# Steps of the RWKV preparation further apart in TensorE's order, key factors ahead of the norm, token mix on ScalarE and VectorE

## The chip, the core and the metric

One core of a Trainium2 chip runs one program. The metric is the device time of one execution in microseconds. Times of parts come from one profiled execution, whose trace names each instruction by its engine and its source line. TensorE (PE) multiplies, VectorE (DVE) and ScalarE (ACT) work on tiles in SBUF and PSUM, GpSimd (POOL) on tiles in SBUF; SyncE (SP) issues the transfers.

## The reference, cut to what matters

One decoder layer over 1024 tokens of width 1024. A normalised input is projected with one wide matrix; its columns feed a windowed attention, an RWKV-7 time mixing and two gates. The part that the change touches is the time mixing:

```python
pr = pr + (pr_prev - pr) * mix            # token mix of r, k, v (pr_prev: the token before)
a = sigmoid(a0 + a_low @ a_up)
kk = k * k_k;  kk = kk / max(norm(kk), 1e-12)      # per head of 64
k = k * (1 + (a - 1) * k_a)
# per token t, per head: S = S diag(decay) + (S @ -kk) (kk*a)^T + v k^T;  y = S @ r
```

The other branch, the merge and the output norm follow, and nothing in them changes.

## The kernel before, in words

The kernel runs in stages: norm and transposition of the input, the RWKV stage (about 97 to 590 us of the trace), attention by head pairs, and the output projections. All large products are made of three fp32r matmuls (high and low halves), hence the lines `acc<-hh,whi`, `acc<-hl,whi`, `acc<-hh,wlo`; their line in the profile is that of the helper `mm`, L140 (transposes: `tr`, L146).

**The RWKV stage** runs the recurrence in 8 segments of 128 tokens, each of two chunks of 64. For each segment there is a preparation (`rwkv_prep`), a rows part (`rwkv_rows`), the chain over the two chunks (`rwkv_chain`, six steps, which depend on one another) and a post part (`rwkv_post`). All are generators: one `next` emits one step. TensorE has a third kind of work in this stage, the projections of spans, gates and of attention-independent columns, cut into units (`run(n)` emits n of them): a unit is one matmul of 512 columns, or two of 256 while the spans last. They fill the time between the dependent steps.

**The order.** While `self.pinned` is set, `mm` and `tr` keep TensorE's instructions in program order, so the order in which `rwkv` calls `next` and `run` is TensorE's order, written out by hand in `PROLOGUE`, `SLOTS` and `FILLS`. The instructions of the other engines and the transfers are not pinned: a planner that simulates the timeline when the kernel is built places them on their queues, and each engine then works in that order. The chain's steps have high priority in it.

In segment i the letters of `SLOTS` mean: `t`, `e`, `a`, `b` the next step of the preparation of segment i, i+1, i+2 and i+3; `f` the rows of segment i+1; `h` the post part of segment i-1. Each slot is one step of the chain, then its letters, then its units (18 in the first six segments, then 14, then 10).

**The steps of a preparation**, between its `yield`s (L498 to L599 and L626 to L668):

1. Load `r` and `k` with the token before (`raw`, L506), mix: POOL subtracts (L508, into tag `cm`), VectorE multiplies and adds (L510), once per head pair.
2. Matmuls of the low-rank codes into two PSUM buffers (`pg`), ScalarE's `tanh` of them (L525: `sig`, `aa`); VectorE's scan of the decay (L530), `kk` and its square `q` on ScalarE (L536, L537).
3. Eight matmuls `pg<-hs,q` for the norms; the power -0.5 on POOL (L545).
4. Transposition of the norms.
5. `pg<-rt,selp`, which spreads the norms; `kk` scaled (L554), exponentials (L558 to L560), `ar` and `bk` on POOL and VectorE (L564 to L571), `k` with its factor (L569, L570), `bw` (L578).
6. and 7. Gram matmuls `pg<-ar,bk` for head pairs 0, 1 and 2, 3: 64 small matmuls into both `pg` buffers, which VectorE masks into `gt` (L592). Step 7 also mixes `v` and sends the blocks of `gt` through DRAM for the inversion of 16x16 blocks on VectorE (`rwkv_blocks`, L601).
8. to 11. The rest of the inverse (`rwkv_inverse`), on `pi` tiles: `pi<-xt,gt`, `pi<-xd,xq`, and the two of 32x32.

The pool `ps_g` of the `pg` tiles has two buffers, and `raw` has two; `k`, `aa`, `cm`, `c` and `bk` have one.

In segment i, `b` makes step 1 of the preparation of segment i+3, `a` steps 2 to 7 of that of i+2, `e` steps 8 to 10 and `t` step 11. In `SLOTS` steps 2 and 3 (`taafh`) follow each other directly, and so do 6 and 7 (`eaa`).

Of the kernel before, what the change touches and what calls it, by code (L numbers as in the profile page):

```python
# [10 lines left out]
F32 = mybir.dt.float32  # L11
# [6 lines left out]
P = 128  # L18
# [5 lines left out]
NPAIR = 4  # L24
# [19 lines left out]

PROLOGUE = (("0", 24), ("0", 10), ("0", 10), ("0", 8), ("0", 44), ("0", 4), ("0", 4), ("1", 12), ("1", 16), ("1", 12),
            ("f", 4), ("f", 4), ("1", 8), ("1", 24), ("0", 8), ("0", 8), ("0", 8), ("1", 0), ("1", 6), ("0", 6), ("2", 0),
            ("f", 8))
SLOTS = ("taafh", "af", "ah", "ef", "eaa", "eb")
FILLS = 6 * [6 * [18]] + [6 * [14], 6 * [10]]
# [61 lines left out]
class Kernel:  # L111
# [233 lines left out]
    def rwkv(self):  # L345
# [5 lines left out]
        with ExitStack() as ctx:  # L351
# [13 lines left out]
            nc.vector.tensor_scalar(self.k_a1, self.k_a, -1.0, 1.0, ALU.mult, ALU.add)  # L365
            self.blk = rc.tile([P, P], F32, name="blk")
# [13 lines left out]
            self.mhalf = rc.tile([P, 1], F32, name="mhalf")  # L380
            nc.vector.memset(self.mhalf, -0.5)
# [40 lines left out]
            def run(n):  # L422
                for _ in range(n):
                    next(fill, None)
# [8 lines left out]
            for i in range(NSEG):  # L433
                chain = self.rwkv_chain(self.segs[i])
                rows = self.rwkv_rows(i + 1) if i + 1 < NSEG else none
                post = self.rwkv_post(self.segs[i - 1]) if i else none
                work = dict(t=prep[i], e=prep[i + 1], a=prep[i + 2], b=prep[i + 3], f=rows, h=post)
                for slot, n in zip(SLOTS, FILLS[i]):
                    with tc.high_priority():
                        next(chain)  # L440
                    for g in slot:
                        next(work[g], None)
                    run(n)
                for n in range(3 * i, 3 * i + 3):
                    self.bias_rows(n)
# [52 lines left out]
    def rwkv_prep(self, s):  # L498
# [5 lines left out]
        def shifted(i, dst):  # L504
            raw = self.rw.tile([P, NPAIR, 1 + SEG], F32, name="raw", tag="raw", bufs=2)
            nc.sync.dma_start(raw, self.raw_d[i].rearrange("p q t -> q p t")[:, :, s * SEG:s * SEG + SEG + 1])  # L506
            d = self.t_("cm")
            nc.gpsimd.tensor_tensor(d, raw[:, :, 0:SEG], raw[:, :, 1:], ALU.subtract)  # L508
            for p in pairs:
                nc.vector.scalar_tensor_tensor(dst[:, p], d[:, p], self.mix[:, 4 * i + p:4 * i + p + 1], raw[:, p, 1:],  # L510
                                               ALU.mult, ALU.add)

        shifted(0, r)
        shifted(1, k)
# [31 lines left out]
        yield  # L546
        self.tr(ps[0:n, 1], rn, self.ident)
        rt = self.rw.tile([n, SEG], F32, name="rt", tag="rt")
        nc.vector.tensor_copy(rt, ps[0:n, 1])
        yield  # L550
        ps = self.ps_g.tile([P, NPAIR, SEG], F32, name="pg", tag="pg")
        for p in pairs:
            self.mm(ps[:, p], self.selp[:, p], rt, start=True, stop=True)
        nc.vector.tensor_tensor(kk, kk, ps, ALU.mult)  # L554

# [5 lines left out]
        nc.vector.tensor_copy(wc, v4(ew)[:, :, :, C - 1:C])  # L561
        ar = self.rw.tile([P, NPAIR, CPS, 2 * C], F32, name="ar", tag="ar", bufs=3)
        bk = self.rw.tile([P, NPAIR, CPS, 2 * C], F32, name="bk", tag="bk")
        nc.gpsimd.tensor_tensor(ar[:, :, :, 0:C], v4(kk), v4(ewm), ALU.mult)  # L564
        nc.gpsimd.tensor_tensor(ar[:, :, :, C:], v4(r), v4(ew), ALU.mult)
        nc.vector.scalar_tensor_tensor(kk, aa, 1.0, kk, ALU.add, ALU.mult)
        nc.vector.scalar_tensor_tensor(bk[:, :, :, 0:C], v4(kk), 0.5, v4(ei), ALU.mult, ALU.mult)
        for p in pairs:
            nc.scalar.activation(aa[:, p], aa[:, p], AF.Identity, bias=col(self.k_a1, p), scale=col(self.k_a, p))  # L569
        nc.gpsimd.tensor_tensor(k, k, aa, ALU.mult)  # L570
        nc.gpsimd.tensor_tensor(bk[:, :, :, C:], v4(k), v4(ei), ALU.mult)  # L571
# [585 lines left out]
```

## Time and profile before

| | us |
|---|---|
| median of three runs | 1474.66 (1471.13 to 1475.28) |
| the profiled execution's own time | 1473.51 |
| its span, first to last instruction | 1471.7 |
| TensorE busy in the span | 1346.3 (91%) |
| VectorE, ScalarE, POOL busy | 795.6, 550.6, 505.3 |
| mean granted TensorE clock | 0.959 |

The time lies 1.8 us above the span, for what is before the first and after the last instruction. An engine's busy time is the union of its instructions' times; issuing and waiting do not count. A granted clock of 1.00 is 2.4 GHz; 0.5 is 1.2 GHz, and a value between is the mean over a stretch at both. Where a row ends in `[1.78 <-ACT sig L525]`, the engine sat idle 1.78 us before it until ScalarE's instruction of line 525 that writes `sig` released it. The segments' chains start at 195.85, 258.07, 316.06, 371.97, 426.05, 483.25, 534.44 and 569.77 us.

### The profile page before, as it was taken

How to read it: one execution, taken by the hardware profiler on the slowest of the kernel's cores; microseconds unless marked ns; L12 is line 12 of the kernel's file. 1: busy time of each engine (PE TensorE's matmuls, PEld its weight loads, DVE VectorE, ACT ScalarE, POOL GpSimd, SP SyncE). 2: the span in 40 equal slices, each digit the busy share in tenths (PEclk: the TensorE clock that was granted, in tenths of full speed). 3: DMA queues.
4: the chain of work that ended last, by engine and by line, in shares of the span. 5: the costliest groups of instructions: out<-in, count | busy, mean ns of one | idle time of the engine just before them, and what ended most of it. 6: DMA issues, size and time to landing. Idle time of an engine off the chain costs nothing.

```text
span 1471.7 us, 25716 instructions
## 1 busy us (share of the span) xinstructions
PE 1346.3 (91%) x10078; PEld 1139.1 (77%) x10078; DVE 795.6 (54%) x1674; ACT 550.6 (37%) x1282; POOL 505.3 (34%) x402
## 2 busy tenths in 40 slices
PE   4988788978988999999999999899989997998997
PEld 3888678867767778788877888788778886776886
DVE  5312535555555552455567656765576558437623
ACT  4444443534533533244433443354325430002211
POOL 1346635634534533322213221322133215344300
PEclk9999889989999999999999999999999998999999
DMA  8673433323223222311122112211131135565216
GB/s 166 163 225 95 121 85 96 91 65 82 77 62 85 67 67 66 88 51 43 39 61 80 36 40 54 87 39 41 47 81 37 36 113 177 179 188 155 80 29 172
DMA packets 199230, 131.17 MB, mean 89 GB/s; under 512 B 52788, under 2 KB 179340, under 8 KB 199108
## 3 DMA queue, kind: packets, MB, share of 16 engines
q1 hardware_dynamic: 199108, 129.52, 32.2%
q8 instruction: 79, 1.29, 0.4%
q14 instruction: 43, 0.35, 0.1%
HBM read 100.31 MB, written 33.89 MB: 91 GB/s over the span
## 4 chain that ended last, share of the span: by engine, by line
PE 38%; DVE 7%; DMA 6%; issue 3%; ACT 3%; POOL 1%; SPq 0%; DVEq 0%; POOLq 0%; ACTq 0%
PE acc L140 24%; DMA wb<-wd 3%; PE acc L1098 2%; PE acc L1097 2%; PE acc L1099 2%; DMA wstage<-in_w_out_dram 1%; PE pw L944 1%; ACT L L877 1%; PE pw L870 1%; PE pw L869 1%; DVE q L848 1%; PE pv L956 1%; PE pv L958 1%; DVE whi L133 1%; PE acc L783 1%
## 5 line engine op out<-in xcount | busy, mean ns | idle before, releaser
L140 PE MATMUL acc<-hh,whi 128*128 128x512 f32 (+1 forms) x1360 | 475.4, 373 | 26.1 <-DVE kl L857 10.8
L140 PE MATMUL acc<-hh,wlo 128*128 128x512 f32 (+1 forms) x1360 | 480.5, 377 | 3.6 <-POOL wlo L136 3.5
L140 PE MATMUL acc<-hl,whi 128*128 128x512 f32 (+1 forms) x1360 | 471.6, 370 | 0.0
L136 POOL TENSOR_TENSOR wlo<-wstage,whi 128x512 fp32r<-128x512 f32 x186 | 249.6, 1342 | 542.7 <-DVE whi L133 255.5
L140 PEld LDWEIGHTS acc<-hh,whi 128*128 128x128 f32 x1360 | 250.7, 194 | 71.4 <-issue 18.7
L140 PEld LDWEIGHTS acc<-hh,wlo 128*128 128x128 f32 x1360 | 251.6, 195 | 44.7 <-POOL wlo L136 5.3
L140 PEld LDWEIGHTS acc<-hl,whi 128*128 128x128 f32 x1360 | 250.4, 194 | 38.1 <-issue 1.3
L877 ACT ACTIVATE L<-L,nm 128x128 f32<-128x128 f32 (+1 forms) x192 | 83.9, 438 | 84.6 <-DVE nm L874 84.4
L871 DVE CUSTOM_DVE_ANT_0 L<-pw,bias 128x128 f32<-128x128 f32 (+1 forms) x192 | 62.4, 351 | 51.2 <-PE pw L870 50.6
L135 ACT CAST whi<-wstage 128x512 fp32r<-128x512 f32 x78 | 48.3, 619 | 107.2 <-PE acc L140 54.2
L856 POOL CAST k<-k 64x512 fp32r<-64x512 f32 x48 | 48.0, 999 | 104.0 <-ACT k L855 97.9
L133 DVE CAST whi<-wstage 128x512 fp32r<-128x512 f32 x108 | 52.5, 487 | 51.9 <-PE acc L140 33.7
L855 ACT CAST k<-acc 64x512 fp32r<-64x512 f32 x48 | 42.9, 894 | 72.9 <-DVE kl L857 51.5
L847 ACT ACTIVATE q<-acc 64x512 fp32r<-64x512 f32 x48 | 43.9, 915 | 57.7 <-DVE q L848 29.6
L857 DVE TENSOR_TENSOR kl<-acc,k 64x512 fp32r<-64x512 f32 x48 | 45.4, 945 | 31.5 <-ACT k L855 31.1
L848 DVE SCALAR_TENSOR_TENSOR q<-acc,q 64x512 fp32r<-64x512 f32 x48 | 44.8, 934 | 21.3 <-ACT q L847 20.4
L947 ACT CAST ph<-pw 128x512 fp32r<-128x512 f32 x72 | 40.8, 582 | 35.2 <-PE pv L956 20.8
L948 DVE TENSOR_TENSOR pl<-pw,ph 128x512 fp32r<-128x512 f32 x72 | 47.3, 670 | 11.8 <-ACT ph L947 10.4
L870 PE MATMUL pw<-kl,q 128*128 128x128 f32 (+1 forms) x192 | 50.7, 278 | 1.4 <-DVE kl L857 1.4
L1097 PE MATMUL acc<-wo,mh 128*128 128x512 f32 x128 | 49.8, 389 | 0.0
L1098 PE MATMUL acc<-wo,mh 128*128 128x512 f32 x128 | 49.8, 389 | 0.0
L1099 PE MATMUL acc<-wo,ml 128*128 128x512 f32 x128 | 49.6, 389 | 0.0
(226 smaller groups left out, 2191.9 us busy)
## 6 DMA issues: line engine op xcount, KB each, us to landing
wstage<-in_w_in_dram SPq DMA_DIRECT2D x170, 256.0 KB
x<-in_x_dram SPq DMA_DIRECT2D x32, 256.0 KB
raw<-raw_d SPq DMA_DIRECT2D x24, 258.0 KB
raw_d<-rv SPq DMA_DIRECT2D x24, 256.0 KB
wb<-wd SPq DMA_DIRECT2D x24, 256.0 KB
bias_d<-bias_r SPq DMA_DIRECT2D x24, 192.0 KB
tb_d<-tb SPq DMA_DIRECT2D x16, 256.0 KB
ga_d<-tb SPq DMA_DIRECT2D x16, 256.0 KB
```

What stands on the lines that cost most here:

```text
L133: self.nc.vector.tensor_copy(hi, x)
L135: self.nc.scalar.copy(hi, x)
L136: self.nc.gpsimd.tensor_tensor(lo, x, hi.bitcast(F32), ALU.subtract)
L140: ins = self.nc.tensor.matmul(*args, **kw)
L848: nc.vector.scalar_tensor_tensor(self.gview(qs2[h][b], g, half), pv, 0.125, hi.bitcast(F32), ALU.mult, ALU.subtract)
L856: nc.gpsimd.tensor_copy(self.gview(ks2[h][b], g, half), hi.bitcast(F32))
L870: nc.tensor.matmul(ps[:, :w], qs2[h][:, qc], kl[h][:, kc], start=False, stop=True)
L871: nc.vector.tensor_tensor_reduce(l[:, l0:l0 + w], ps[:, :w], self.bias[h][:, bo:bo + w], 1.0, -3.0e38, ALU.add, ALU.max, st[:, gi, 0, h, n ...
L877: nc.scalar.activation(ls, ls, AF.Exp, bias=nm[:, n:n + 1], scale=1.0, accum_out=st[:, gi, 1, h, n:n + 1])
L1097: nc.tensor.matmul(ps, mh[k][:, ts], wh[:, k], start=k == 0, stop=False)
L1098: nc.tensor.matmul(ps, mh[k][:, ts], wl[:, k], start=False, stop=False)
L1099: nc.tensor.matmul(ps, ml[k][t // 4][:, cs], wh[:, k], start=False, stop=k == KT - 1)
```

## The change

It does four things. `SLOTS` becomes `LOOP`, a list of (what, units), where `C` is a step of the chain; the units are multiplied by `FILLS`, 6 in the first six segments, then 5, then 3. The six steps of the chain keep 18 x 6 units per segment between them, and the steps of the preparations are spread over them. In the prologue four units are added ahead of step 7 of the second preparation. In step 1 `k` comes before `r`, and the mix is `(1 - mix) * raw` on ScalarE and then `mix * raw_before + that` on VectorE; POOL's subtraction goes. The exponentials move to step 3, and `k`'s factor (into tag `c`, no longer over `aa`), `k`, its half of `bk` and `r`'s half of `ar` move to step 4, ahead of the spreading of the norms.

```diff
-            ("f", 4), ("f", 4), ("1", 8), ("1", 24), ("0", 8), ("0", 8), ("0", 8), ("1", 0), ("1", 6), ("0", 6), ("2", 0),
+            ("f", 4), ("f", 4), ("1", 8), ("1", 24), ("0", 8), ("0", 8), ("0", 8), ("1", 4), ("1", 6), ("0", 6), ("2", 0),
...
-SLOTS = ("taafh", "af", "ah", "ef", "eaa", "eb")
-FILLS = 6 * [6 * [18]] + [6 * [14], 6 * [10]]
+LOOP = (("C", 0), ("t", 0), ("f", 1), ("a", 1), ("h", 1), ("C", 0), ("f", 1), ("a", 2), ("C", 0), ("a", 1), ("h", 2),
+        ("C", 0), ("a", 1), ("f", 0), ("e", 2), ("C", 2), ("a", 1), ("e", 0), ("C", 1), ("a", 1), ("e", 1), ("b", 0))
+FILLS = 6 * [6] + [5, 3]
...
+            self.mix1 = rc.tile([P, 12], F32, name="mix1")
+            nc.vector.tensor_scalar(self.mix1, self.mix[:, 0:12], -1.0, 1.0, ALU.mult, ALU.add)
...
-                for slot, n in zip(SLOTS, FILLS[i]):
-                    with tc.high_priority():
-                        next(chain)
-                    for g in slot:
+                for g, n in LOOP:
+                    if g == "C":
+                        with tc.high_priority():
+                            next(chain)
+                    else:
                         next(work[g], None)
-                    run(n)
+                    run(n * FILLS[i])
...
-            d = self.t_("cm")
-            nc.gpsimd.tensor_tensor(d, raw[:, :, 0:SEG], raw[:, :, 1:], ALU.subtract)
             for p in pairs:
-                nc.vector.scalar_tensor_tensor(dst[:, p], d[:, p], self.mix[:, 4 * i + p:4 * i + p + 1], raw[:, p, 1:],
-                                               ALU.mult, ALU.add)
-
+                nc.scalar.activation(dst[:, p], raw[:, p, 1:], AF.Copy, scale=self.mix1[:, 4 * i + p:4 * i + p + 1])
+            for p in pairs:
+                nc.vector.scalar_tensor_tensor(dst[:, p], raw[:, p, 0:SEG], self.mix[:, 4 * i + p:4 * i + p + 1],
+                                               dst[:, p], ALU.mult, ALU.add)
+
+        shifted(1, k)
         shifted(0, r)
-        shifted(1, k)
...
-        yield
-        self.tr(ps[0:n, 1], rn, self.ident)
-        rt = self.rw.tile([n, SEG], F32, name="rt", tag="rt")
-        nc.vector.tensor_copy(rt, ps[0:n, 1])
-        yield
-        ps = self.ps_g.tile([P, NPAIR, SEG], F32, name="pg", tag="pg")
-        for p in pairs:
-            self.mm(ps[:, p], self.selp[:, p], rt, start=True, stop=True)
-        nc.vector.tensor_tensor(kk, kk, ps, ALU.mult)
-
         ew, ewm, ei = self.t_("q"), cm, self.t_("sig")
...
         nc.vector.tensor_copy(wc, v4(ew)[:, :, :, C - 1:C])
+        yield
+        self.tr(ps[0:n, 1], rn, self.ident)
+        rt = self.rw.tile([n, SEG], F32, name="rt", tag="rt")
+        nc.vector.tensor_copy(rt, ps[0:n, 1])
         ar = self.rw.tile([P, NPAIR, CPS, 2 * C], F32, name="ar", tag="ar", bufs=3)
         bk = self.rw.tile([P, NPAIR, CPS, 2 * C], F32, name="bk", tag="bk")
+        t = self.t_("c")
+        for p in pairs:
+            nc.scalar.activation(t[:, p], aa[:, p], AF.Identity, bias=col(self.k_a1, p), scale=col(self.k_a, p))
+        nc.gpsimd.tensor_tensor(k, k, t, ALU.mult)
+        nc.gpsimd.tensor_tensor(bk[:, :, :, C:], v4(k), v4(ei), ALU.mult)
+        nc.gpsimd.tensor_tensor(ar[:, :, :, C:], v4(r), v4(ew), ALU.mult)
+        yield
+        ps = self.ps_g.tile([P, NPAIR, SEG], F32, name="pg", tag="pg")
+        for p in pairs:
+            self.mm(ps[:, p], self.selp[:, p], rt, start=True, stop=True)
+        nc.vector.tensor_tensor(kk, kk, ps, ALU.mult)
         nc.gpsimd.tensor_tensor(ar[:, :, :, 0:C], v4(kk), v4(ewm), ALU.mult)
-        nc.gpsimd.tensor_tensor(ar[:, :, :, C:], v4(r), v4(ew), ALU.mult)
         nc.vector.scalar_tensor_tensor(kk, aa, 1.0, kk, ALU.add, ALU.mult)
         nc.vector.scalar_tensor_tensor(bk[:, :, :, 0:C], v4(kk), 0.5, v4(ei), ALU.mult, ALU.mult)
-        for p in pairs:
-            nc.scalar.activation(aa[:, p], aa[:, p], AF.Identity, bias=col(self.k_a1, p), scale=col(self.k_a, p))
-        nc.gpsimd.tensor_tensor(k, k, aa, ALU.mult)
-        nc.gpsimd.tensor_tensor(bk[:, :, :, C:], v4(k), v4(ei), ALU.mult)
```

`mhalf`, the constant -0.5, is also made a few lines earlier.

## Rows read from the trace of the kernel before

**Rows 1.** Table by stretch: us, busy PE, PEld, DVE, ACT, POOL, clock, DMA, GB/s.

```profile
195.85:534.44 338.59, 298.32 (x3765) 255.08 (x3764) 185.18 (x421) 150.12 (x360) 158.54 (x130) 0.90 0.30 78
...
534.44:569.77 35.33, 33.84 (x423) 27.35 (x422) 15.03 (x45) 13.78 (x33) 10.74 (x10) 1.00 0.23 66
614.60:1471.70 857.10, 814.28 (x4092) 678.30 (x4092) 509.93 (x1026) 288.91 (x706) 234.96 (x176) 0.98 0.28 81
```

**Rows 2.** Waits of TensorE, 195.85 to 534.44: us in total, times, longest.

```profile
PE pg L140 <- DVE gt L592: 22.2, 9, 4.5
PE pg L140 <- ACT sig L525: 15.0, 6, 3.2
```

**Rows 3.** Timeline of TensorE, 374 to 380: start, us, instruction, idle before.

```profile
374.54 1.71 PE L140 MATMUL pg<-wa,waup 64*128 64x128 f32 x16
378.03 1.05 PE L140 MATMUL pg<-hs,q 128*128 128x2 f32 x8 [1.78 <-ACT sig L525]
```

**Rows 4.** Timeline of ScalarE, same stretch.

```profile
376.32 0.63 ACT L752 ACTIVATE yt<-d 128x512 f32<-128x512 f32 x1 [0.93 <-DVE d L751]
376.85 1.12 ACT L525 ACTIVATE sig<-pg,vecs 128x128 f32<-128x128 f32 x4
```

**Rows 5.** Timeline of TensorE, 406 to 415.

```profile
406.25 0.68 PE L140 MATMUL upd<-rhs_s,tt 64*64 64x64 f32 x16
406.76 1.10 PE L140 MATMUL pi<-xd,xq 64*64 64x64 f32 x32
407.69 1.17 PE L140 MATMUL pg<-ar,bk 64*64 64x64 f32 x64
412.29 0.33 PE L140 MATMUL pg<-ar,bk 64*64 64x64 f32 x2 [3.43 <-DVE gt L592]
412.89 1.66 PE L140 MATMUL pg<-ar,bk 64*64 64x64 f32 x62 [0.27 <-DVE gt L592]
```

**Rows 6.** Timeline of VectorE, 407 to 413 and 437 to 439.

```profile
407.85 2.13 DVE L510 SCALAR_TENSOR_TENSOR k<-cm,vecs,raw 128x128 f32<-128x128 f32 x4 [1.15 <-POOL cm L508]
...
411.58 1.25 DVE L592 TENSOR_TENSOR gt<-pg,gmask 128x512 f32<-128x512 f32 x2
...
437.61 0.71 DVE L641 STREAM_TRANSPOSE xt<-xd 128x512 f32<-128x512 f32 x1 [1.21 <-DMA xd<-x_d]
```

**Rows 7.** Same table, projection matmuls and users of `acc` alone.

```profile
332.32:336.61 4.29, 4.29 (x18) 3.28 (x18) 0.69 (x1) 0.09 (x1) 1.00 0.16 61
379.67:385.38 5.71, 5.71 (x18) 4.33 (x18) 0.69 (x1) 0.60 (x1) 0.73 0.30 82
...
215.96:220.45 4.49, 4.49 (x36) 4.35 (x36) 0.00 (x0) 0.00 (x0) 1.00 0.45 129
```

**Rows 8.** Groups of TensorE, 97 to 600: busy us, mean ns, idle before.

```profile
L140 PE MATMUL pg<-rt,selp 8*128 8x128 f32 x64 | 9.2, 283 | 0.0
```

**Rows 9.** Tile raw: ns min/median/max of its users; idle time of their engines before them.

```profile
L510 DVE SCALAR_TENSOR_TENSOR r<-cm,vecs,raw x32: 335/1123/1380, 89.1 to 461.7; 128x128 f32<-128x128 f32 x32
...
L508 POOL TENSOR_TENSOR cm<-raw x24: 1040/1042/1547, 88.0 to 510.1; 128x512 f32<-128x512 f32 x24
...
  POOL cm L508: 55.8, 11
  DMA raw<-raw_d: 11.6, 3
```

**Rows 10.** Line L573, a 128x128 product on ScalarE: ns min/median/max.

```profile
L573 ACT ACTIVATE r<-r,vecs x32: 385/387/404, 119.3 to 497.0; 128x128 f32<-128x128 f32 x32
```

**Rows 11.** Timeline of SP's queue and of POOL, from 139.5.

```profile
139.62 0.92 SPq L506 DMA_DIRECT2D raw<-raw_d  x2
...
143.11 1.04 POOL L508 TENSOR_TENSOR cm<-raw 128x512 f32<-128x512 f32 x1 [5.53 <-DMA raw<-raw_d]
```

**Rows 12.** Waits of TensorE, 97 to 195.85.

```profile
PE pg L140 <- ACT q L537: 14.3, 2, 8.6
```

**Rows 13.** Timeline of ScalarE, from 139.5.

```profile
153.50 1.02 ACT L536 ACTIVATE kk<-k,vecs 128x128 f32<-128x128 f32 x3 [6.95 <-DVE k L510]
```

More of the change, by code (lines that the diff above doesn't have):

```diff
@@ L365, in rwkv @@
             nc.vector.tensor_scalar(self.k_a1, self.k_a, -1.0, 1.0, ALU.mult, ALU.add)
+            self.mhalf = rc.tile([P, 1], F32, name="mhalf")
+            nc.vector.memset(self.mhalf, -0.5)
+            self.mix1 = rc.tile([P, 12], F32, name="mix1")
+            nc.vector.tensor_scalar(self.mix1, self.mix[:, 0:12], -1.0, 1.0, ALU.mult, ALU.add)
             self.blk = rc.tile([P, P], F32, name="blk")
@@ L379, in rwkv @@
             nc.vector.tensor_copy(self.selp, ps[0:2 * NPAIR])
-            self.mhalf = rc.tile([P, 1], F32, name="mhalf")
-            nc.vector.memset(self.mhalf, -0.5)
             self.smask = rc.tile([P, NPAIR * SEG], F32, name="smask")
```

## The prediction

> **What bounds the kernel now.** I read the table by stretch first. TensorE does most of the work, so time can only come from its idle gaps or from a slow clock, and the table says where these are. From 614.6 us to the end it is busy 814 of 857 us at a granted clock of 0.98. In the six segments from 195.85 to 534.44 us it is busy 298 of 338.6 us, at 0.90 [rows 1]. The segment after them, in which no preparation step 2 to 7 runs, has 1.5 us of idle time and a clock of 1.00. The list of TensorE's waits names two causes for the six segments [rows 2]: the Gram matmuls behind L592's masking on VectorE (22.2 us in the six segments, nearly one wait a segment, longest 4.5) and the norm's matmuls behind L525's evacuation on ScalarE (15.0, six times, longest 3.2). That is 37.2 us.
>
> Both are places where the fixed order puts a step straight behind the one that feeds it. In the segment from 371.97, step 2's 16 matmuls end at 376.25 and step 3 starts at 378.03 with nothing between them [rows 3]: ScalarE came to `sig` at 376.85, after an `ACTIVATE` of the post step that had waited for VectorE [rows 4]. Step 6's Gram group ends at 408.86, and step 7's waits 3.43 us and again 0.27 [rows 5]. The masking it waits for starts at 411.58, and VectorE spent the time before on the token mix of a later preparation, `k` from 407.85 after 1.15 us on POOL [rows 6], and on three short steps behind it.
>
> A wait costs twice. The same 18 fill units take 4.29 us at granted 1.00 and 5.71 at 0.73, in the stretch just behind the wait of step 3 [rows 7]: part of it ran at the lower level, 1.2 GHz.
>
> **The target.** The segment from 534.44 shows the undisturbed price: 35.33 less its 1.5 us of idle time [rows 1] is 33.83 with 84 units. A full segment has 24 units more, 24 x 0.238 = 5.72, and the steps 2 to 7: 1.71 and 1.05 [rows 3], the norm's spreading 9.2/8 = 1.15 [rows 8], two Gram groups at 1.17 [rows 5]. That makes 45.8. The first two segments' units cost 4.49 a slot, not 4.29 [rows 7], so 1.2 more each. Six segments: 277 of today's 338.6. **At most 62 us** is to be had in them: 37.2 of waits, 25 mostly of slow clock.
>
> **The change, part by part.**
> *Order.* The units per segment stay 18 x 6; the last two segments trade six units (84 to 90, 60 to 54). Nothing is added to TensorE. Between steps 2 and 3 now lie 12 units (2.86), `upd` (0.68 [rows 5]), four transposes and 6 units (1.43): 5.0 us without the transposes, against a longest wait of 3.2. Between steps 6 and 7 lie 6 units, step 9 (1.10 [rows 5]), the chain's third step (two groups of 16 like `upd`, about 1.3, an estimate) and 6 units: 5.3 us against a longest wait of 4.5. Both waits go, the second with less to spare. The chain's own six steps stay 18 units apart. What comes later relative to its use is the block inverse: in today's trace its result is transposed at 437.61, 23 us after the Gram group's end at 414.55 [rows 5, 6]. In the new order 72 units (17.1 us) and some 12 us of small groups (an estimate from their rows) lie before step 8, which reads it, so it stays hidden with some 6 us to spare. Step 7 takes its transfers along on SP's queue, `v`'s load, two stores and four loads of blocks, then four stores and two loads, nearer to step 1's loads. At 0.46 us an issue [rows 11] that is 6 us in 23; the weights are asked for a whole projection ahead, which hides it from TensorE. Without that lead it would cost up to the 6.
> *Key factors ahead of the norm.* They move three POOL products and four ScalarE steps from after the norm's spreading to before it. Step 6 does not wait in the trace, so this is worth nothing by itself; it keeps step 6 safe now that it comes sooner. If POOL took them ahead of the `pow`, step 4's transpose would wait 3 to 5 us (three 128x512 steps at 1.04 to 1.55 [rows 9]) less 4 of cover; the `pow` needs only the norm's matmuls and is ready before the exponentials' users, so I take nothing.
> *Token mix.* Out go 24 POOL subtractions (1.04 to 1.55 us), in come 96 ScalarE products of 128x128 at 0.387 us [rows 9, 10]: 12 a segment, 4.6 us. ScalarE was busy 150 of 338.6 us [rows 1]; it goes to (150 + 28)/283 = 63%. VectorE keeps its 96 steps, but they no longer stand behind POOL, for which it sat idle 55.8 us in all, and the longer of them (median 1.12 us for `r` against a shortest of 0.335 [rows 9]) may shrink. None of this lies on TensorE's path; it takes the token mix's waiting on POOL out of what delays the masking. The raw loads remain 24 and only their order changes, `k` first; SP passes the same queue. A ScalarE product can now stand waiting for a load: about 3.5 us from issue to the first use [rows 11], with the chain's copies behind it. The bounds are nothing and 3.5 us per shift; the chain's steps lie some 6 us apart, so I take nothing on the path but keep 1 us a segment for all such leftovers, 6 us.
> The 96 products are 37 us of ScalarE; if all of it reached TensorE, the sum below would be 1443, which is a harder form of rival 1 and has its chance there. A rule of the Trainium skill speaks for that side: ScalarE: Activation LUTs, Rules for kernel authors, sends multiplies and adds to VectorE, not to ScalarE. The trace does not bear it out for these shapes, since VectorE's own steps of the token mix are the dear ones (median 1.12 us against 0.387).
> *Prologue* (97 to 195.85 us). TensorE waits 14.3 us in two norm steps [rows 12]. The second, 8.6, is on `kk`, for which ScalarE sat idle 6.95 us [rows 13]: `k`'s load is third, behind `v` and `r`, which share two buffers. With `k` ahead of `r` I take 6 us (between 3 and 8.6). The first, 5.7, waits for a load that cannot come earlier; one POOL step less and a better order on ScalarE give 2 (0 to 4.5). Shorter waits return some 3 us of slow clock (2 to 5). Together 11, between 3 and 18.
> *Sum:* 62 - 6 + 11 = 67. The profiled execution took 1473.5 us (span 1471.7), 1.2 below the median of 1474.66. **1473.5 - 67 = 1406 us.** What follows this stage is bound by TensorE and moves up with it.
>
> **The rivals.**
> 1. *ScalarE takes over as the one that is late.* `sig`, `aa`, `kk`, the square, the post step and the products come to some 8 us of it around steps 2 and 3 (two times 1.12, two times 0.63 [rows 4], twelve times 0.387 [rows 10]), and a load's 3.5 us may come on top. If step 3 still waits 2 us a segment and the clock falls with it (1.4 in the fill and about as much in the small groups), 6 x 4.8 = 29 us stay: 1435. For it: today's wait is one of ScalarE's order. Against: 5 us of cover.
> 2. *The masking stays late: the change does not do what it says.* Only TensorE's order is written out; the planner places VectorE's work, and it did put the token mix before the masking [rows 6]. If the masking comes 2 us beyond the cover, 2 us and about 2 of clock in six segments: 1430. Against: POOL's waits in that queue are gone.
> 3. *Slower than before.* ScalarE's products wait for all three loads in a row with the chain's copies behind: 3 x (3.5 + 4 x 0.387) = 15 us less 6 of cover is 9 us of idle TensorE, with 3 of slow clock 12 a segment. In eight segments 96 us, more than the 67: 1406 + 96 = 1502. It decides from about 12 us of blocked ScalarE a segment, where 6 of idle time and 2 of clock, eight times, eat the 67. For it: VectorE stood 55.8 us behind the same loads' users [rows 9], and ScalarE kept its order when `yt` was not ready and `sig` stood behind it [rows 4]. The Trainium skill has this as a rule, in TensorE: Matmul & The Clock Gate, section Architectural detail: ScalarE's queue is a strict FIFO; the trace agrees. Against: the loads were mostly there when POOL came to them (it waited for one 3 times in 24 [rows 9]).
>
> **How the numbers follow.** Forecast 0.62; rival 1 0.16, rival 2 0.10, rival 3 0.04; the rest, in which smaller leftovers add up differently, 0.08. The forecast's own range is 1393 (no leftovers, the prologue's best) to 1420; 7 us below it are left for the later stages, which run at 0.98 [rows 1]. Rivals 1 and 2 reach to 1440, so the range is **1386 to 1440**. Faster by over 0.3% (4.4 us, about what a measurement of this kernel can tell from no change): 0.91; within it 0.04; slower 0.05.
>
> **What would show it.** Right: in the changed profile the two rows of TensorE waits on L525 and L592 are gone from the loop, its granted clock there is near 1.00, six segments take about 47 us each instead of 51 to 62, and from then on every stage takes what it took. Rival 1 would show TensorE waiting for `sig` or `q`, ScalarE idle on raw loads; rival 2 the old wait on the masking; rival 3 waits in the chain's `rhs`, `upd` and `snew`. The prediction is wrong if a new wait of over 2 us a segment stands in the loop, or if the later stages, which it counts at no change, move by more than a few us.

## The result and the profile after

The changed kernel takes **1425.85 us** (median of four runs, 1425.36 to 1427.3) against 1473.35 for the one before, measured beside it (four runs, 1471.13 to 1475.28). The ratio is 0.968, 95% interval 0.9662 to 0.9697. The forecast was 1406 with a range of 1386 to 1440: the sign and the mechanism hold, the gain is 47.5 us where 67 were expected.

The profiled execution has a span of 1425.5 us (before: 1471.7). Three rows of its table by stretch answer to [rows 1], with the same columns: the six full segments, the segment behind them, and the last 857.1 us.

```profile
194.87:488.01 293.14, 282.28 (x3760) 231.90 (x3759) 169.59 (x413) 164.20 (x420) 138.38 (x115) 0.99 0.34 89
488.01:525.10 37.09, 35.89 (x429) 28.29 (x429) 14.36 (x45) 15.04 (x35) 10.29 (x9) 1.00 0.26 70
568.40:1425.50 857.10, 815.10 (x4092) 678.92 (x4092) 507.63 (x1026) 289.04 (x707) 237.53 (x177) 0.98 0.28 81
```

Six segments went from 338.59 to 293.14 us, and the clock in them from 0.90 to 0.99. That is 45.5 of the 46.2 us by which the span shrank. The prologue ahead of them gave 1.0 (195.85 to 194.87), and everything behind them took 0.2 more (937.26 to 937.49). The last 857 us show the same busy times as before, as forecast.

TensorE's waits in the six segments, in us in total, times, longest (answers to [rows 2]):

```profile
PE pg L148 <- POOL rn L550: 7.6, 6, 1.9
PE pg L142 <- DVE kk L573: 2.2, 2, 1.9
PE snew L142 <- ACT uv L732: 0.9, 2, 0.6
```

Both rows of [rows 2], 37.2 us, are gone: nothing waits for the masking or for `sig`. In their place stand 10.7 us of three new waits, above all for the power of the norms (`rn`), once a segment. The same list for the prologue from 97 us (answers to [rows 12]):

```profile
PE pg L142 <- ACT q L542: 8.6, 2, 5.8
PE pg L142 <- DVE rt L560: 5.4, 1, 5.4
```

The waits for `q` fell from 14.3 to 8.6 (5.76 and 2.81), and a wait for the transposed norms (`rt`) took 5.4 back.

**What the new waits are.** In the segment from 293.45 the norms' eight matmuls end at 306.06. The timeline of VectorE says when it came to them (start, us, instruction, idle before):

```profile
299.49 0.17 DVE L624 TENSOR_TENSOR xtmp<-xinv 64x14 f32<-64x14 f32 x1 [7.89 <-DMA xinv<-tin_d]
...
305.11 0.98 DVE L624 TENSOR_TENSOR xtmp<-xinv 64x56 f32<-64x56 f32 x1
306.13 1.22 DVE L626 TENSOR_TENSOR xinv<-xinv,xtmp 64x56 f32<-64x56 f32 x1
...
310.57 0.17 DVE L626 TENSOR_TENSOR xinv<-xinv,xtmp 64x14 f32<-64x14 f32 x1
310.66 0.15 DVE L549 TENSOR_SCALAR rn<-pg 128x8 f32<-128x8 f32 x1
```

The timeline of all engines from 309.9 shows how it goes on at GpSimd and TensorE:

```profile
309.95 0.68 PE L142 MATMUL rhs<-uv,gt 64*64 64x64 f32 x16
...
310.89 1.64 POOL L550 TENSOR_TENSOR rn<-rn,mhalf 128x8 f32<-128x8 f32 x1 [3.61 <-DVE rn L549]
...
312.58 0.27 PE L148 MATMUL pg<-ident,rn 128*8 128x128 f32 x1 [1.95 <-POOL rn L550]
```

VectorE's queue is worked in order, and the planner put the 28 short steps of the block inversion (`xtmp`, `xinv`) ahead of the norms. The first of them sat 7.89 us waiting for its load, the norms' evacuation came 4.60 us after it could have (306.06 to 310.66), and the power added 1.64. In the prologue the copy `rt` runs at 165.34, right behind the last `xinv` step, though what it copies was ready at 158.39.

### The profile page after: what moved, and what is told of

The parts are those of the page before. It is cut to its first block, busy times and chain, and to the rows that moved or that the text cites. A ratio compares the mean times of both kernels' runs of the same rounds, so it can differ in the third digit from the quotient of the medians.

```text
span 1425.5 us, 25770 instructions
## 1 busy us (share of the span) xinstructions
PE 1334.2 (94%) x10078; PEld 1118.8 (78%) x10078; DVE 780.5 (55%) x1675; ACT 575.4 (40%) x1378; POOL 477.4 (33%) x378
## 5 line engine op out<-in xcount | busy, mean ns | idle before, releaser
L142 PE MATMUL acc<-hh,wlo 128*128 128x512 f32 (+1 forms) x1360 | 469.8, 369 | 2.0 <-POOL wlo L138 1.9
L142 PEld LDWEIGHTS acc<-hh,whi 128*128 128x128 f32 x1360 | 247.7, 192 | 70.8 <-issue 16.9
L142 PEld LDWEIGHTS acc<-hh,wlo 128*128 128x128 f32 x1360 | 247.6, 192 | 41.1 <-POOL wlo L138 3.7
L142 PEld LDWEIGHTS acc<-hl,whi 128*128 128x128 f32 x1360 | 247.5, 192 | 35.3 <-issue 1.7
L624 DVE TENSOR_TENSOR xtmp<-xinv 64x14 f32<-64x14 f32 (+6 forms) x112 | 33.5, 299 | 44.4 <-DMA xinv<-tin_d 41.5
L853 DVE SCALAR_TENSOR_TENSOR q<-acc,q 64x512 fp32r<-64x512 f32 x48 | 44.8, 933 | 20.9 <-ACT q L852 20.1
L952 ACT CAST ph<-pw 128x512 fp32r<-128x512 f32 x72 | 40.8, 583 | 36.0 <-PE pv L961 19.4
L875 PE MATMUL pw<-kl,q 128*128 128x128 f32 (+1 forms) x192 | 50.6, 278 | 1.4 <-DVE kl L862 1.4
```

What stands on the lines that cost most here:

```text
L142: ins = self.nc.tensor.matmul(*args, **kw)
L875: nc.tensor.matmul(ps[:, :w], qs2[h][:, qc], kl[h][:, kc], start=False, stop=True)
```

## Which part did what: the change in pieces

The change has three separable parts: the **order** (`LOOP`, `FILLS`, the prologue's four units), the **mix** (token mix on ScalarE and VectorE, `k` first) and the **keys** (exponentials and key factors ahead of the norm). Five kernels hold some of them and not the others; each is the diff of the change, cut to its part. The kernel before took 1475.05 to 1477.2 us beside the kernels of this and the following sections, and 1473.35 beside the changed kernel. By medians these kernels therefore stand some 2 to 4 us too high against the changed one; the ratios are free of this.

*The new order alone:*

```diff
-SLOTS = ("taafh", "af", "ah", "ef", "eaa", "eb")
+LOOP = (("C", 0), ("t", 0), ("f", 1), ("a", 1), ("h", 1), ("C", 0), ("f", 1), ("a", 2), ("C", 0), ("a", 1), ("h", 2),
...
```

> The kernel before with the new order and unit counts alone (LOOP, FILLS, PROLOGUE); POOL's subtraction, r before k and the late key factors stay. Theory: the distance between the steps is what takes the two waits away. Before, the masking of step 6 ended at most 4.5 us after its Gram group, the norm's buffer came at most 3.2 us late; 5 us now lie between. So the waits on L525 and L592 in the six segments fall from 37 us to under 4, their slow clock goes with them, and the time is near the changed kernel's: 1426 to 1436 us. Rival: the order alone fails because VectorE's masking stays behind the token mix that waits on POOL and gets later as the segments get shorter: waits on L592 stay at 10 us or more and the time at 1445 us or more.

Measured: 1451.94 us (1448.87 to 1456.32), ratio 0.9844 [0.9819, 0.987]. The time is the rival's, its reason is not: the masking is waited for 2.1 us in the six segments, so the order does what it says and gains too little by it.

*The token mix alone:*

```diff
-            nc.gpsimd.tensor_tensor(d, raw[:, :, 0:SEG], raw[:, :, 1:], ALU.subtract)
...
+                nc.scalar.activation(dst[:, p], raw[:, p, 1:], AF.Copy, scale=self.mix1[:, 4 * i + p:4 * i + p + 1])
```

> The kernel before with the new token mix alone (products on ScalarE, k before r); old order, old key factors. Theory: TensorE's 15.0 us of waits on L525 stay within 3 us, since nothing comes between steps 2 and 3; the waits on L592 fall from 22.2 us to about 9 (two maskings of 0.68 us and the way to them, 1.5 us a segment), since the mix of the next preparation no longer waits on POOL ahead of the masking. With its slow clock some 20 us: 1448 to 1460 us. Rival A: the mix is worth nothing by itself: 1470 to 1476. Rival B: ScalarE's 4.6 us a segment make the waits on L525 longer: 1476 or more.

Measured: 1469.28 us (1466.43 to 1473.42), ratio 0.9961 [0.9945, 0.9977]: hardly more than can be told from no change, and no less masking wait. The theory's 1448 to 1460 did not come.

*The key factors alone* (steps 3 and 4 as in the changed kernel, old order, old mix):

```diff
+        nc.gpsimd.tensor_tensor(k, k, t, ALU.mult)
+        nc.gpsimd.tensor_tensor(bk[:, :, :, C:], v4(k), v4(ei), ALU.mult)
+        nc.gpsimd.tensor_tensor(ar[:, :, :, C:], v4(r), v4(ew), ALU.mult)
+        yield
         ps = self.ps_g.tile([P, NPAIR, SEG], F32, name="pg", tag="pg")
...
```

> The kernel before with the key factors, k and the exponentials ahead of the norm's spreading alone; old order, old mix. Theory: step 6 never waited, so nothing is gained: 1469 to 1477 us, the waits on L525 and L592 as before within 4 us. Rival: less POOL work between steps 5 and 6 lets the masking and the token mix come earlier on VectorE, the waits on L592 fall by a third or more: 1455 to 1465 us.

Measured: 1471.42 us (1462.2 to 1475.98), ratio 0.9961 [0.994, 0.9981], in total as small as expected. The waits did not stay as they were, though: the rival's fall of the masking wait came without its time. The table below shows two large effects of opposite sign.

*Order and mix* (the changed kernel with steps 3 to 5 as before):

> The changed kernel with the key factors back where they were (after the norm's spreading). Theory: they are worth nothing here either: 1422 to 1432 us (changed kernel 1425.85). Rival: step 6 comes sooner in the new order and now waits for bk: 2 us or more of waits a segment behind L567's and L571's values, 1436 us or more.

Measured: 1439.73 us (1437.03 to 1441.05), ratio 0.9753 [0.973, 0.9776]. The two parts without the third do not make the change: 13.9 us are missing (10.8 by the ratios), which the keys bring. The rival's time came and its reason did not: no wait for `bk` is listed.

*Order and keys* (the changed kernel with the old mix):

> The changed kernel without its token mix: GpSimd subtracts and VectorE multiplies and adds as before, the new order and the early key factors stay. If the parts add up (the new order alone gave 1451.9 us, and the key factors took 14 us from order plus mix, 1439.7 to 1425.9), 1436 to 1442 us. Rival: the subtractions and the key factors' products stand in the one queue of GpSimd, so that what the key factors win is lost again by the values arriving late; then 1446 us or more, with the prologue up to the first segment longer than the 197.8 us of the new order alone, as it grew by 10 us (196.9 to 207.0) when the key factors alone were put into the kernel before.

Measured: 1449.88 us (1443.25 to 1452.9), ratio 0.9819 [0.9789, 0.985], which cannot be told from the order alone. The sum does not hold, and the prologue grew as the rival said (196.7 to 204.3).

From the profiled execution of each, where the time lies (prologue to the first segment's chain, the six segments, what follows; TensorE's waits in the six):

| parts | span | prologue | six segments | rest | masking | `sig` | others |
|---|---|---|---|---|---|---|---|
| none (before) | 1471.7 | 195.9 | 338.6 | 937.3 | 22.2 | 15.0 | 2.7 |
| mix | 1466.5 | 190.5 | 337.1 | 938.9 | 23.6 | 15.6 | 1.6 |
| keys | 1468.6 | 206.0 | 325.7 | 936.9 | 12.0 | 23.0 | 2.4 |
| order | 1449.8 | 196.7 | 314.2 | 938.9 | 2.1 | 2.1 | 19.2 |
| order, mix | 1439.3 | 190.8 | 308.1 | 940.4 | 1.7 | 0.5 | 17.4 |
| order, keys | 1441.5 | 204.3 | 301.6 | 935.7 | 0 | 0 | 14.9 |
| all (after) | 1425.5 | 194.9 | 293.1 | 937.5 | 0 | 0 | 10.7 |

These are single executions. The one of order and keys lies 6.6 us below the median of its own runs (1443.25 against 1449.88), so its row flatters it; the others lie within 1.5 us of their medians. Among the four rows with the new order nothing was changed in what follows the six segments, and it still differs by up to 4.8 us; differences of that size in a column carry little weight.

**Read by columns**, each part has its own place. The order removes the two old waits by itself, as argued, but gains 24.4 us in the six segments and not 56, because 19.2 us of other waits come up. The mix gains 5.3 to 9.4 us in the prologue and only 1.5 in the six segments while the old order stands (6.1 and 8.4 with the new). The keys gain 12.6 to 15.0 us in the six segments with either order, and cost the prologue 10.1 with the old order and mix, 7.5 with the new order, 4.1 with both.

**What the keys do alone** shows in one group of VectorE's, the mix of `r` in the six segments (xcount, busy us, mean ns, idle before). Before:

```profile
L510 DVE SCALAR_TENSOR_TENSOR r<-cm,vecs,raw 128x128 f32<-128x128 f32 x24 | 23.1, 1017 | 0.0
```

With the keys alone:

```profile
L513 DVE SCALAR_TENSOR_TENSOR r<-cm,vecs,raw 128x128 f32<-128x128 f32 x24 | 6.8, 338 | 0.0
```

The same 24 instructions take a third of the time. In the segment of [rows 5] GpSimd's products for `bk`, `r` and `bw` ran beside them; now GpSimd is idle there, and the masking that stood behind these steps is waited for 12.0 us where it was 22.2 [rows 2]. That is not the whole gain of 12.9 us. The wait for `sig` grew by 8.0, for a reason that no run shows, so TensorE's idle time fell by 3.0 us only; the other 9.9 are TensorE's busy time, 298.32 to 288.41 us, at a clock of 0.94 where it was 0.90 [rows 1]:

```profile
205.96:531.68 325.72, 288.41 (x3764) 246.66 (x3763) 171.05 (x423) 149.62 (x360) 159.70 (x132) 0.94 0.32 81
```

**What they do inside the change** is in part another thing. Of the 15.0 us that they take from order and mix in the six segments, 13.8 lie in the first and the third (56.2 to 48.1 and 56.3 to 50.6 us). Among the waits that went there are those for `uv`, with order and mix 6.0 us in the six segments. The longest of them, in the first segment (timelines of VectorE, ScalarE and TensorE):

```profile
227.78 3.98 DVE L515 SCALAR_TENSOR_TENSOR r<-raw,vecs,r 128x128 f32<-128x128 f32 x4 [1.00 <-ACT r L513]
...
236.19 0.99 ACT L513 ACTIVATE v<-raw,mix 128x128 f32<-128x128 f32 x3 [4.32 <-DMA raw<-raw_d]
237.20 0.37 ACT L732 COPY uv<-upd 64x256 f32<-64x256 f32 x1
...
237.62 0.69 PE L142 MATMUL snew<-uv,bkt 128*64 128x64 f32 x16 [1.99 <-ACT uv L732]
```

The mix of `r` runs beside GpSimd's `bk`, `r` and `bw` (227.99 to 232.65) and takes 3.98 us. `raw` has two buffers, and the next loads into them start at 231.78 and 234.64, right behind the mixes of `r` and `k` (ends 231.76 and 234.61). So `v` comes late, ScalarE's product of `v` stands waiting for it, and the chain's copy `uv` stands behind that product. This is the queue of the prediction's rival 3: five such waits of ScalarE, 16.0 us in the six segments with order and mix, and none in the changed kernel. The chain is read from the timeline; no run isolates it.

**Why the keys cost the prologue** is the same thing seen from the other side: what GpSimd's products now run beside is the block inversion. Of VectorE's timeline in the changed kernel:

```profile
157.65 0.20 DVE L624 TENSOR_TENSOR xtmp<-xinv 64x54 f32<-64x54 f32 x1
157.88 1.18 DVE L626 TENSOR_TENSOR xinv<-xinv,xtmp 64x54 f32<-64x54 f32 x1
...
160.62 1.30 DVE L624 TENSOR_TENSOR xtmp<-xinv 64x44 f32<-64x44 f32 x1
161.96 1.19 DVE L626 TENSOR_TENSOR xinv<-xinv,xtmp 64x44 f32<-64x44 f32 x1
...
165.34 0.27 DVE L560 COPY rt<-pg 8x128 f32<-8x128 f32 x1
```

GpSimd's in the same stretch, back to back from 159.23 to 164.31:

```profile
159.23 1.29 POOL L566 TENSOR_TENSOR k<-k,c 128x512 f32<-128x512 f32 x1 [0.23 <-ACT c L565]
160.60 1.26 POOL L567 TENSOR_TENSOR bk<-k,sig 128x512 f32<-128x512 f32 x1
161.82 1.26 POOL L579 TENSOR_TENSOR r<-r,k 128x512 f32<-128x512 f32 x1
```

And VectorE with order and mix, where these products come later:

```profile
160.07 0.20 DVE L624 TENSOR_TENSOR xtmp<-xinv 64x44 f32<-64x44 f32 x1
...
161.70 0.27 DVE L554 COPY rt<-pg 8x128 f32<-8x128 f32 x1
```

A step of 64x44 takes 0.20 us alone and 1.30 beside a product, and each slow step is about as long as one GpSimd instruction (1.18 to 1.30 against 1.26 to 1.33). The last two also end just behind it, at 161.92 and 163.15 against 161.86 and 163.08. These rows look like one engine standing still for the length of the other's instruction, not like two that share a bandwidth. The Trainium skill says so in SBUF — State Buffer, section SBUF: two separate sides: the port pair that VectorE and GpSimd share is locked for a whole instruction, between VectorE's steps with two inputs in SBUF, among others, and GpSimd's instructions that read SBUF, and the loser blocks. The rows above agree with it. `rt` comes at 165.34 instead of 161.70; with order and mix alone no wait for it is listed. In the two kernels with the keys and the old mix the prologue's new wait is another, 4.1 and 4.3 us for `xq`, and no run shows its cause.

## Is it VectorE's block inversion? Leaving it out, and going around it

*Thirteen of its fourteen elimination steps left out*:

```diff
-        for j in range(1, 15):
+        for j in range(1, 2):
```

> The changed kernel with 13 of the 14 elimination steps of the block inversion left out (26 of 28 VectorE instructions a segment; every load and store of it stays). Theory: the block inversion in VectorE's queue is what holds up the norms; TensorE's waits for L550 and L560 fall from 13.0 us to 2 or less, the key wait L573 and the uv wait go too, and the time is 1408 to 1418 us. Rival: the block only stands there, and GpSimd's queue is what is late (its products and the power); the waits stay at 8 us or more and the time at 1421 us or more.

Measured: 1420.66 us (1417.29 to 1421.58), ratio 0.963 [0.961, 0.965]. TensorE's waits from 97 us to the end of the six segments:

```profile
PE pg L142 <- ACT q L542: 8.7, 2, 5.4
PE pg L142 <- DVE kk L573: 4.0, 2, 2.3
PE pg L148 <- POOL rn L550: 2.9, 1, 2.9
PE snew L142 <- ACT uv L732: 2.0, 2, 1.5
```

The waits for L550 and L560 fell from 13.0 to 2.9 us, near the 2 that the theory gave, and the prologue shrank to 187.1. But the time fell by 5 us (7 by the ratios) and not by 8 to 18. In the profiled execution, the fastest of the four, 7.8 us of the gain lie in the prologue and 0.6 in the six segments: `kk` and `uv` grew by 2.9 us, and the first segment took 52.5 us instead of 48.1. The table by stretch of its last three full segments (46.50, 46.50 and 46.90 us) carries the best price of a segment that any run has:

```profile
339.80:386.30 46.50, 46.50 (x610) 36.95 (x609) 20.92 (x45) 27.29 (x72) 21.37 (x19) 1.00 0.35 91
...
432.80:479.70 46.90, 46.90 (x610) 37.30 (x609) 15.72 (x31) 21.89 (x55) 22.59 (x19) 1.00 0.29 78
```

TensorE, whose work this run does not touch, is busy for all of it at full clock: **46.5 us is the floor of a segment in this order**.

*The norms around VectorE's queue:* evacuation, `rt` and VectorE's half of `uv` on ScalarE:

```diff
-        nc.vector.tensor_scalar(rn, ps[:, 0, 0:n], 1e-24, None, ALU.max)
+        nc.scalar.activation(rn, ps[:, 0, 0:n], AF.Identity, bias=self.tiny, scale=1.0)
...
-        nc.vector.tensor_copy(rt, ps[0:n, 1])
+        nc.scalar.copy(rt, ps[0:n, 1])
...
-            nc.vector.tensor_copy(uv[own[0], :, 1, ch], ps[own[0]])
+            nc.scalar.copy(uv[own[0], :, 1, ch], ps[own[0]])
```

> The changed kernel with three small steps taken off VectorE's queue: the norms' evacuation (plus 1e-24 in place of the larger of it and 1e-24), the copy of the transposed norms and VectorE's half of the uv copy, all on ScalarE. Theory: TensorE's waits left in the changed kernel (L550 7.6 us, L560 5.4 us, L732 0.9 us between 95 and 490 us, 13.9 in all) come from these standing behind the block inversion in VectorE's queue; they fall to 3 us or less in all, and with the clock that a wait costs the time is 1408 to 1418 us. Rival A: GpSimd's power and its products ahead of it make the norms late; the wait for L550 stays at 5 us or more and the time at 1421 us or more. Rival B: ScalarE is now late with its other work; 1426 us or more, with new waits for ScalarE.

Measured: 1427.99 us (1421.27 to 1435.63), ratio 0.9679 [0.9638, 0.9719], the same as the changed kernel. The wait for `rt` fell from 5.4 to 1.5 and that for `uv` went, but that for the power grew from 7.6 to 9.7. ScalarE's timeline says why; the norms' matmuls ended at 303.45:

```profile
305.09 0.63 ACT L556 ACTIVATE cm<-cm 128x512 f32<-128x512 f32 x1 [2.47 <-POOL cm L538]
305.73 0.47 ACT L688 ACTIVATE bkt<-pg,sgn 128x256 f32<-128x256 f32 x1
...
307.41 0.60 ACT L137 CAST whi<-wstage 128x512 fp32r<-128x512 f32 x1
308.04 0.27 ACT L551 ACTIVATE rn<-pg,tiny 128x8 f32<-128x8 f32 x1
```

The planner put an exponential ahead of the norm that waits for GpSimd, so the norm came 4.59 us late in another queue. Rival A's numbers came true, with ScalarE's order as the reason; GpSimd has its part in it through `cm`, for which that exponential waited 2.47 us. The profiled execution was 2.8 us ahead of the changed kernel's at the end of the six segments and lost 5.0 behind them.

*The block inversion behind the norms* in VectorE's queue. A copy from the norms into the steps' scratch ties it there, and the inversion gets a place of its own in the loop's order and in the prologue's:

```diff
+        yield
         tm = self.rw.tile([nb * nm, 64], F32, name="xtmp", tag="xtmp", bufs=1)
+        if self.rn is not None:
+            nc.vector.tensor_copy(tm[:, 0:1], self.rn[0:nb * nm, 0:1])
...
-("f", 1), ("a", 2), ("C", 0)
+("f", 1), ("a", 0), ("e", 2), ("C", 0)
```

> The changed kernel with the 28 steps of the block inversion placed behind the norms' evacuation in VectorE's queue (a copy of 64 values from the norms into the steps' scratch holds them there; loads, stores and all other work stay, TensorE's order too). If the norms wait for that inversion alone, as the run that left most of it out says, the waits for L550 and L560 of the changed kernel (7.6 and 5.4 us) fall to 3 us or less together without giving anything up: 1412 to 1421 us. Rival: the inversion ends some 3 to 5 us later, its result misses the inverse's first product, and TensorE waits for that (xt) instead, 5 us or more over the loop; 1425 us or more.

Measured: 1502.57 us (1497.31 to 1504.21), ratio 1.017 [1.0145, 1.0195], slower than the kernel before. The waits for L550 and L560 did go (0.6 us for `rt` is left), and these came, from 97 us to the end of the six segments:

```profile
PE pi L142 <- DVE xt L652: 25.9, 7, 13.2
PE pg L148 <- DVE kk L575: 17.7, 5, 5.2
PE pg L142 <- ACT ys L774: 14.6, 5, 4.6
```

VectorE's timeline shows that the edit moved the inversion by more than meant:

```profile
335.02 0.17 DVE L550 TENSOR_SCALAR rn<-pg 128x8 f32<-128x8 f32 x1 [0.30 <-PE pg L142]
339.75 0.83 DVE L558 COPY wc<-q 128x8 f32<-128x8 f32 x1 [4.57 <-ACT q L555]
340.50 0.13 DVE L625 COPY xtmp<-rn 64x1 f32<-64x1 f32 x1
340.67 1.16 DVE L630 TENSOR_TENSOR xtmp<-xinv 64x14 f32<-64x14 f32 x1
```

The copy stands behind `wc`, which waits for an exponential, and so the inversion starts 5.5 us after the norms, beside GpSimd's products (its first step takes 1.16 us for 0.17). How a clean move right behind the norms would do stays open. What the run shows is the other side of the trade: the inversion's early place costs 13 us of norm waits, and a late one costs several times that, because the next segment's `xt` and `kk` stand behind it.

## Is it slack? Moving fill to where TensorE waits

Three kernels keep every instruction and shift only units of fill.

*In the loop*, one piece from behind to ahead of the norms' transposition:

```diff
-("a", 2), ("C", 0), ("a", 1), ("h", 2),
+("a", 2), ("C", 1), ("a", 1), ("h", 1),
```

> The changed kernel with one piece of fill in the loop's order moved from behind the transposition after the norms' to ahead of the norms' own (6 units in each of the six segments, 1.6 us). Theory: the waits for L550 (7.6 us in six, none over 1.9) are a matter of TensorE coming 1 to 2 us too early to a norm that VectorE's block inversion holds up; 1.6 us of work ahead of it fills them, 2 us or less of L550 stay, nothing else grows, and the time is 1416 to 1421 us. Rival: the steps behind it (the copy of the norms, the key wait L573) come that much closer, and what goes at L550 returns there; 1423 to 1430 us.

Measured: 1431.73 us (1424.0 to 1436.37), ratio 0.9693 [0.9669, 0.9718]; its interval overlaps the changed kernel's, and the gain of 5 to 10 us that the theory gave did not come. Its waits in the six segments:

```profile
PE pg L142 <- DVE kk L573: 7.2, 3, 2.7
PE pg L142 <- DVE rt L560: 2.8, 3, 1.3
PE snew L142 <- ACT uv L732: 0.9, 3, 0.4
PE pg L148 <- POOL rn L550: 0.4, 1, 0.4
```

The wait for `rn` went from 7.6 to 0.4 and came back whole at `kk` and `rt`: 11.3 us in all where there were 10.7. The rival's mechanism was right, its time just below the measured one: the chain norm, power, transposition, spreading, `kk` has a length of its own.

*In the prologue*, 52 units moved ahead of the three waits:

```diff
-PROLOGUE = (("0", 24), ("0", 10), ("0", 10), ("0", 8), ("0", 44), ("0", 4), ("0", 4), ("1", 12), ("1", 16), ("1", 12),
-            ("f", 4), ("f", 4), ("1", 8), ("1", 24),
+PROLOGUE = (("0", 24), ("0", 32), ("0", 10), ("0", 8), ("0", 22), ("0", 4), ("0", 4), ("1", 12), ("1", 26), ("1", 12),
+            ("f", 4), ("f", 4), ("1", 28), ("1", 24),
...
```

> The changed kernel with fill in the prologue's order moved to where it waits: 22 units from behind the first norm broadcast to ahead of the first norm (wait 5.8 us), 10 more ahead of the second (2.8 us) and 20 more ahead of the second broadcast (5.4 us); 30 of these are taken from what is left at the end of the fill. Theory: all three are TensorE arriving early in a fixed order; of 14.0 us 4 or less stay, and with the clock that they cost (0.89 over the last 86 us of the prologue) the time is 1408 to 1417 us. Rival: the chain of the second segment's preparation is as long as it is, so that a new wait stands right behind (the inverse's first step, the products with the masks); 1420 us or more.

Measured: 1445.18 us (1441.05 to 1447.13), ratio 0.9783 [0.9763, 0.9802], 19 us worse than the changed kernel (15 by the ratios). The waits for `q` and `rt` are gone from the prologue, and its list reads

```profile
PE pg L142 <- DVE gt L597: 3.4, 1, 3.4
PE acc L142 <- POOL wlo L138: 3.3, 2, 1.9
PE acc L142 <- ACT rv L479: 2.1, 1, 2.1
...
```

With two shorter ones that is 11.6 us, part of them now the fill's own (its weights `wlo`, its evacuation `rv`). The six segments took 304.6, and at the end of the stage, where the borrowed units are missing, TensorE waits 11.4 us for the attention's `q` (L853), where the changed kernel waits 2.5.

*Both moves:*

> Both moves of fill at once. If the waits left in the changed kernel are all of one kind (TensorE early by 1 to 6 us in a fixed order, each a thing of its own), their gains add: 1400 to 1412 us. Rival: with the waits ahead gone everything in the loop comes earlier against the loads and VectorE's queue, and waits for the inverse or the key return; 1414 us or more.

Measured: 1449.88 us (1444.64 to 1454.18), ratio 0.9816 [0.9794, 0.9837]. Nothing adds.

## Has ScalarE room?

Every product of the token mix computed twice:

```diff
             for p in pairs:
-                nc.scalar.activation(dst[:, p], raw[:, p, 1:], AF.Copy, scale=self.mix1[:, 4 * i + p:4 * i + p + 1])
+                for _ in range(2):
+                    nc.scalar.activation(dst[:, p], raw[:, p, 1:], AF.Copy, scale=self.mix1[:, 4 * i + p:4 * i + p + 1])
```

> The changed kernel with every one of ScalarE's 96 products of the token mix computed twice over: 12 more a segment at 0.387 us, 4.6 us of ScalarE in a segment of 48.9. Theory: ScalarE has the room (27.2 us busy in such a segment) and what it makes is early enough, so 1424 to 1431 us, TensorE's waits for ScalarE in the loop at most 4 us in all. Rival (the prediction's first: ScalarE is what is late next): 1436 us or more, with waits of TensorE for uv, sig or bkt of 10 us or more.

Measured: 1440.98 us (1436.98 to 1448.08), ratio 0.977 [0.9737, 0.9804]: 15 us more (13 by the ratios) for 37 us of products. The time is the rival's, the waits for ScalarE in the six segments are nearer to the theory's (4.8 us). In the prologue

```profile
PE pg L142 <- ACT q L543: 19.5, 2, 10.0
```

stands where 8.6 stood, and the first segment takes 52.9 us instead of 48.1. The other five differ by -1.9 to +1.0. ScalarE has room in the loop and none in the prologue, where its products lie in the chain that TensorE waits for.

## Why the prediction was right in kind and 20 us short

**Right.** The two waits of [rows 2] were the bound, the new order alone removes them (22.2 and 15.0 us to 2.1 each), the clock returned with them (0.90 to 0.96 with the order alone, 0.99 with all parts), and the later stages did not move. Rival 2, a masking that stays late, has no trace in the changed kernel. Rival 3 did not come in it: in the six segments ScalarE waited for no raw load, in the prologue three times (5.8, 4.6 and 0.7 us), and the chain's waits for its copies are 0.9 us. Its mechanism was real, though: with order and mix alone it is the 16.0 us of ScalarE shown above, and the keys, counted at nothing, took it away.

**Wrong, term by term** (executions of [rows 1] and of the result):
- *The target, 45.8 us a segment.* "Nothing is added to TensorE" is true of its instructions, not of its time: the wait-free floor is 46.5. 6 x 0.7 = 4.2 us. The 108 units are now in 13 pieces of 6 or 12 instead of 6 pieces of 18. The timelines bear this out as the reason: taken from the start of each piece to the start of the next group, the pieces of the segment from 339.8 take 27.1 us (1.48 to 1.59 for 6 units, 2.94 to 2.97 for 12), where the sum had 26.4 (20.66 in the segment of 84 units, and 5.72); all other groups take 19.4 in both.
- *Leftovers, 1 us a segment.* 10.7 us, 1.8 a segment: 4.7 us more. The step that failed is "the block inverse stays hidden": it was examined for its own result and not for what stands behind it in VectorE's queue. The new order brought the norms to where its 28 steps run. Some 1 us of slower clock (0.99) comes on top.
- *The prologue, 11 us.* 1.0. The second `q` wait fell by 5.8 as argued (the mix alone takes the prologue from 195.9 to 190.5). The first stayed at 5.76, where 2 had been taken off. The rest was given back by the keys, through GpSimd's products beside the inversion and the wait for `rt`.
- *Key factors, "worth nothing by itself".* By themselves they give 0.4%, within the change they are worth 13.9 us (1439.73 to 1425.85; 10.8 by the ratios). The question put to the trace was whether step 6 waits for GpSimd's products; it had to be what runs beside them. [rows 9] held a good part of the answer, the median of 1.12 us against a shortest of 0.335 for `r`: it was read as a cost of the mix, though the products next to it made it.
- *Masking waits, "nearly one wait a segment".* [rows 2] has nine in six segments. No term of the sum hangs on it.
- *Token mix, "none of this lies on TensorE's path".* 12.2 us inside the new order (1451.94 to 1439.73), of which 5.9 lie in the prologue, where 6 had been counted, and 6.1 in the six segments, where nothing had. By the rule of the Trainium skill that the prediction weighed (ScalarE: Activation LUTs, Rules for kernel authors) this multiply belongs on VectorE. The prediction read the trace against it, and that reading was wrong: without GpSimd beside it VectorE's step takes 0.338 us, less than ScalarE's 0.387. What is measured is that ScalarE in the place of GpSimd's subtraction gains; no run has the multiply on VectorE.

So the sum had the parts on the wrong accounts. It gave the order 56 of its 67 us, on the assumption that what is idle in the six segments goes when the two waits go. Alone the order gives 24, for 19.2 us of other waits come up behind the two, and the mix and the keys bring the other 26 (1451.94 to 1425.85; 24 by the ratios). That the time still lies in the forecast's range is in part luck: parts that the sum counted at nothing in the six segments stood in for the one that fell short.

Rival 1 (ScalarE late) holds in one place of the changed kernel only, the prologue's first `q`, and its 1435 for the loop did not come.

No run beat the changed kernel with its whole computation: loop_shift and norm_uv_act cannot be told from it. Leaving out most of the inversion gains 5 us (7 by the ratios), as the planner then places the rest.

## What to carry to other kernels

When a step is moved on one engine, read the queue of every engine that serves it at its new place: here the two waits that went were replaced by queue neighbours that had been harmless before. Where the mean of an instruction lies far above its shortest time (here 1.02 against 0.34 us), look for what runs beside it; here moving that neighbour was worth as much as moving the instruction. And a wait in a fixed order is only slack if the chain behind it is short: shifting fill to it is a cheap test, and here the wait came back further on.

## What the runs showed that had not been expected

- A VectorE step of 0.17 to 0.20 us takes 1.16 to 1.30 beside a 128x512 instruction of GpSimd. In the prologue's chain of 28 such steps (147.7 to 165.4 us) eight were stretched so.
- A wait of 1 to 2 us need not cost clock. Before, the stretch behind a wait of 1.78 us showed 0.73 [rows 3, 7]. The changed kernel has six waits for `rn` of up to 1.95 us, and five of its six segments show 1.00. With order and mix three waits of 1.1 to 2.3 us within the first segment (`bv`, `bkt`, `uv`) go with 0.91 and a segment of 56.2 us instead of 48.1.
- Kernels differ in scatter. The changed one repeats within 2 us (1425.36 to 1427.3), the one with the norms on ScalarE within 14 (1421.27 to 1435.63), on nearly the same computation and waits.
